# Attention's filler keeps two Strassen products of each of eight gate pairs, and sums of products accumulate in PSUM

## The chip, the cores and the metric

One core of one Trainium2 chip. The metric is the device time of one launch in microseconds (us). The core's engines run side by side, each through its own instruction list in a fixed order, and wait for each other by semaphores: TensorE (PE, with its weight loads shown as PEld), VectorE (DVE), ScalarE (ACT), GpSimd (POOL) and SyncE (SP, which here issues DMAs). Matrix products land in PSUM banks of 128 x 512 fp32 numbers; DVE and ACT read them from there.

## The reference, cut to what matters

```python
def encoder_layer(x, ...):                        # a prompt of 512 tokens, then a sample of 1024
    h = rmsnorm(x, norm_g)
    proj = h @ w_in                               # 1024 -> 4352 + 1024 columns
    qa, ka, va, za, qb, kb, vb, zb, ga, gb = split(proj)
    oa = neighbourhood_attention(qa, ka, va, rpb_a) * silu(za) @ w_o_a   # (after q, k norms)
    ob = window_gqa_attention(qb, kb, vb, t5_table, sink_b) * silu(zb) @ w_o_b
    merged = sigmoid(ga) * oa + sigmoid(gb) * ob  # ga, gb: 1024 columns each
    return x + merged @ w_out
```

Everything is fp32. `z` below stands for za and zb, "gates" for ga and gb, "out" for the product with w_out.

## The kernel before, in words

Everything is kept transposed, with features on the 128 partitions and tokens along the free axis. Two batches follow each other: the prompt (0 to about 395 us) and the sample (from there to the end). The change concerns the sample, which has four stages: attention (about 396 to 785 us), z and the gates (785 to 960), the merge, which multiplies with w_o and the gates (960 to 1083), and out (1083 to the end).

**Precision.** An fp32 operand is split into a rounded part (hi, made by ACT) and a remainder (lo, source minus hi, made by DVE or POOL). `product` (L1276) multiplies a weight block with 512 tokens over k: for each of four k-steps three matmuls of 512 columns, hi x hi (L1284), hi x lo (L1285) and lo x hi (L1286). A product of half of k is thus 12 matmuls into one bank. In the profile `hh`, `hl` are h's parts, `whi`, `wlo` the weights', `fh`, `fl` the filler's weights, and `T` the parts of sums of blocks of h.

**Pairs in Strassen form.** Two blocks of 128 output features by two halves of the tokens by two halves of k make a 2x2 block product. `pair_strassen` (L1320) computes it in seven products (Strassen's scheme in Winograd's form) instead of eight. Products 0 and 1 take plain blocks of weights and of h. Products 2 to 6 need four sums of weights (`S`, 512 columns each, L1161) or the four sums T0 to T3 of h; product 6 takes a sum of weights and plain h. In before each product goes into its own bank; then ACT copies product 0 out (L1354, `U`), and DVE adds (L1161, `U<-U,x` and `C<-U,x`) join the products in SBUF: three partial sums and four results, seven adds in a pair. Results get their sigmoid from ACT (L1387) and are stored in DRAM (`g_d`). In the sample three z pairs, six gate pairs and two out pairs have this form; the rest is plain.

**Sums of h.** T0 to T3 are computed at the start, where the norm is (`norm_pair`), and stored in `t_d`; the dense stage loads them as `U` and splits them into `T` (`stored_sums`, L1237, L1167 and L1172), in the order T1, T2, T0, T3.

**The filler.** Attention leaves gaps on PE while its softmax runs. `fill_gates` fills them with gate products of four of the sixteen gate blocks, two halves of the tokens each: 8 products over the whole k, 24 matmuls each, into one bank `d` that serves the filler alone in this stage. ACT or DVE drains the bank into the one buffer `fc` (L1493), which is stored in `g_d` (L1394). These blocks' pairs are left out of the gates stage; the sigmoid follows when the merge loads them.

**Order.** Nothing is scheduled at run time. A planner (`Flow.run`) takes each operation with a cost, a priority and what it depends on, simulates the engines and writes the operations out in the order of that plan; `f.value` gives a tile from a ring of a stated number of buffers, and a new tile waits until the readers of the one that had the buffer are done. Dense products rotate over eight banks (`ROTA`: two `p`, five `x`, one `d`).

Of the kernel before, what the change touches and what calls it, by code (L numbers as in the profile page):

```python
# [25 lines left out]
FILL_P, FILL_S = 3, 2  # L26
# [14 lines left out]
P = 128  # L41
# [313 lines left out]
def encoder_kernel(  # L355
# [207 lines left out]
    def norm_pair(pool, x_t, rb, hh, hl, t, t_d, prio, load_prio):  # L563
# [572 lines left out]
    def dense_phase(geo, hh, hl, h_ops, o_stores, exps_done, start, opened, tp, up, p0, p1, p2, x_t, y_t, classic, fill, after_gates=None, side=None):  # L1136
# [10 lines left out]
        g_d = dpool.tile([2, 8, P, nt], F32, tag=f"g_d{nt}", name=f"g_d{nt}")  # L1147
        stores = {}
# [36 lines left out]
        def sums(prio, done):  # L1185
# [3 lines left out]
            for k in range(4):  # L1189
# [27 lines left out]
                step(3, lambda v=t[1]: v.t[:, :sn], (1, 0), 0, ALU.subtract, True, t[1])  # L1217
                step(3, lambda v=t[3]: v.t[:, :sn], (1, 0), 1, ALU.subtract, False)
# [57 lines left out]
        def product(ps, ws, movs, prio, first, last, after=(), n=nh):  # L1276

            o = None
            for k, ((hi, lo, c, wops), (mh, ml, mops, mv)) in enumerate(zip(ws, movs)):

                def emit(e, k=k, hi=hi, lo=lo, c=c, mh=mh, ml=ml):
                    out = ps.t[:, :n]
                    cs = slice(c, c + P)
                    pe.matmul(out, hi.t[:, cs], mh(), start=first and k == 0, stop=False)  # L1284
                    pe.matmul(out, hi.t[:, cs], ml(), start=False, stop=False)  # L1285
                    pe.matmul(out, lo.t[:, cs], mh(), start=False, stop=last and k == len(ws) - 1)  # L1286
# [33 lines left out]
        def pair_strassen(srcs, post, prio, mov_h, mov_t, seed=None, last=False):  # L1320
# [19 lines left out]
            def add(out, x, bank, op=ALU.add):  # L1340
                tt(pv(out), pv(x), pv(bank), op, sn, prio, psum=True, new=[out], use=[x, bank])

            def result(m, n, x, bank, op=ALU.add):
                if seed:
                    c = seed(m, n * sn, sn, x, prio)
                    tt(pv(c), pv(c), pv(bank), op, sn, prio, psum=True, use=[c, bank], into=[c])
                else:
                    c = tile_("C", n_c)
                    add(c, x, bank, op)
                post(m, n * sn, sn, c, False, prio)  # L1350

            a = mul(0, mov_h(0, 0))
            f.op(
# [9 lines left out]
            if not last:  # L1363
                result(0, 1, u4, mul(6, mov_h(1, 1)))
                return
# [406 lines left out]
```

## Time and profile before

| | before |
|---|---|
| median of 3 runs (lowest, highest) | 1146.3 us (1145.42, 1147.29) |
| span of the profiled execution | 1144.7 us |
| PE, PEld, DVE, ACT, POOL busy, whole span | 99%, 86%, 75%, 56%, 27% |
| granted clock of TensorE, every slice | 9 or more tenths |
| DMA moved | 159.86 MB, 140 GB/s in the mean |

The profile is of one execution and gives its span from the first to the last instruction; of its own time it shows nothing beyond that span. The span lies 1.6 us under the median of the runs; that much of a launch is outside it. PE's busy time counts from the start of a matmul to its modelled end, so that matmuls overlap and a busy PE isn't yet PE at its peak: what one matmul costs is read from the distance of two starts. "Idle before" and "waited for" are the engine's time with nothing to do, and what ended it.

### The profile page before, as it was taken

To read this page: it belongs to the slowest core of one execution; us is meant where nothing else is said; L and a number is where in the kernel's file an instruction comes from. 1 tells how busy PE (TensorE), PEld (TensorE's weight loads), DVE (VectorE), ACT (ScalarE), POOL (GpSimd) and SP (SyncE) were. 2 spreads that over 40 slices of the span, in tenths; PEclk is the share of its full clock that TensorE was granted. 3 is DMA by queue.
4 is the path that set the end of the run, shared out by engine and by line. 5 is a ranking of instruction groups with operands and counts; after the bars stand their busy time and mean duration, and the time that the engine had idled before them with its cause. 6 is when DMAs were issued, how large, how long until landed. Compare 5 with 4: busy or idle time off the path is not lost.

```text
span 1144.7 us, 18482 instructions
## 1 busy us (share of the span) xinstructions
PE 1133.8 (99%) x6139; PEld 985.8 (86%) x6139; DVE 854.4 (75%) x1975; ACT 644.9 (56%) x1467; POOL 308.3 (27%) x413
## 2 busy tenths in 40 slices
PE   8999999999999999999999999999999999999998
PEld 6999988888888899999999888888888888788887
DVE  5888798497765468887778888865878755497984
ACT  5777987544433346665678988865534434343320
POOL 3653433000010054343333445330222210132110
PEclk9999999999999999999999999999999999999999
DMA  7854543488786422121221213226657335573072
GB/s 253 273 158 141 181 113 102 115 264 266 232 277 199 165 72 67 25 70 32 71 61 50 56 37 93 56 66 214 218 148 211 129 111 159 200 238 121 29 223 90
DMA packets 124705, 159.86 MB, mean 140 GB/s; under 512 B 28297, under 2 KB 66961, under 8 KB 124610
## 3 DMA queue, kind: packets, MB, share of 16 engines
q1 hardware_dynamic: 124610, 158.69, 45.4%
q8 instruction: 48, 0.79, 0.3%
q14 instruction: 47, 0.39, 0.1%
HBM read 121.93 MB, written 41.44 MB: 143 GB/s over the span
## 4 chain that ended last, share of the span: by engine, by line
PE 94%; DVE 2%; DMA 2%; ACT 1%; POOL 1%; issue 0%; SPq 0%; ACTq 0%; POOLq 0%
PE p L761 25%; PE x L1285 9%; PE x L1286 9%; PE x L1284 9%; PE x L1063 5%; PE x L1026 5%; PE x L934 4%; PE p L1284 4%; PE p L1285 4%; PE d L1284 4%; PE p L1286 4%; PE d L1286 4%; PE d L1285 4%; PE x L861 2%; DMA ot<-u_d 1%; DMA w<-in_w_att_dram 1%
## 5 line engine op out<-in xcount | busy, mean ns | idle before, releaser
L761 PE MATMUL p<-whi,hh 128*128 128x384 f32 x384 | 133.4, 348 | 0.0
L761 PE MATMUL p<-wlo,hh 128*128 128x384 f32 x384 | 133.1, 347 | 0.0
L761 PE MATMUL p<-whi,hl 128*128 128x384 f32 x384 | 132.4, 345 | 0.0
L978 ACT ACTIVATE sb<-sb,mx 128x384 f32<-128x384 f32 (+1 forms) x192 | 107.5, 563 | 22.4 <-DVE mx L969 22.2
L1167 ACT ACTIVATE whi<-raw 128x512 fp32r<-128x512 f32 (+1 forms) x140 | 81.1, 590 | 52.6 <-PE x L1285 26.2
L761 PE MATMUL p<-whi,hb 128*128 128x384 f32 x384 | 107.5, 347 | 0.0
L1172 POOL TENSOR_TENSOR wlo<-raw,whi 128x512 fp32r<-128x512 f32 (+1 forms) x29 | 40.9, 1413 | 242.4 <-ACT whi L1167 130.4
L1284 PE MATMUL x<-hh,whi 128*128 128x512 f32 x264 | 102.7, 389 | 0.0
L1285 PE MATMUL x<-hl,whi 128*128 128x512 f32 x264 | 102.7, 389 | 0.0
L1286 PE MATMUL x<-hh,wlo 128*128 128x512 f32 x264 | 102.7, 389 | 0.0
L1037 DVE TENSOR_TENSOR pp<-x,pp 128x512 fp32r<-128x512 f32 (+1 forms) x136 | 82.6, 638 | 18.9 <-ACT pp L1032 17.8
L1172 DVE TENSOR_TENSOR wlo<-raw,whi 128x512 fp32r<-128x512 f32 (+1 forms) x111 | 70.1, 645 | 30.5 <-ACT whi L1167 30.2
L1285 PE MATMUL x<-T,whi 128*128 128x512 f32 x224 | 87.5, 390 | 0.3 <-DVE T L1172 0.2
L1286 PE MATMUL x<-T,wlo 128*128 128x512 f32 x224 | 87.2, 389 | 0.0
L1284 PE MATMUL x<-T,whi 128*128 128x512 f32 x224 | 87.1, 389 | 0.0
L1032 ACT ACTIVATE pp<-x 128x512 fp32r<-128x512 f32 (+1 forms) x136 | 70.9, 560 | 22.8 <-PE x L1026 21.8
L799 POOL TENSOR_TENSOR rs_r<-rs_v,mhalf 128x4 f32<-128x4 f32 (+1 forms) x72 | 81.7, 1134 | 5.7
L1063 PE MATMUL x<-pp,v 128*128 128x256 f32 (+1 forms) x368 | 77.8, 324 | 0.8 <-DVE pp L1037 0.8
L792 POOL TENSOR_SCALAR rs_v<-ss 128x4 f32<-128x4 f32 (+1 forms) x72 | 26.2, 364 | 187.3 <-DVE ss L785 184.6
L761 PEld LDWEIGHTS p<-whi,hl 128*128 128x128 f32 x384 | 73.0, 190 | 1.3 <-issue 1.0
L761 PEld LDWEIGHTS p<-wlo,hh 128*128 128x128 f32 x384 | 73.0, 190 | 1.0 <-issue 0.5
L761 PEld LDWEIGHTS p<-whi,hh 128*128 128x128 f32 x384 | 73.0, 190 | 0.9 <-issue 0.5
(351 smaller groups left out, 2985.5 us busy)
## 6 DMA issues: line engine op xcount, KB each, us to landing
raw<-in_w_g_dram SPq DMA_DIRECT2D x76, 256.0 KB
w<-in_w_att_dram SPq DMA_DIRECT2D x46, 384.0 KB
ot<-o_d SPq DMA_DIRECT2D x36, 256.0 KB
g_d<-C SPq DMA_DIRECT2D x34, 256.0 KB
raw<-in_w_z_dram SPq DMA_DIRECT2D x32, 256.0 KB
raw<-in_w_out_dram SPq DMA_DIRECT2D x32, 256.0 KB
C<-g_d SPq DMA_DIRECT2D x24, 256.0 KB
out_dram<-C SPq DMA_DIRECT2D x23, 256.0 KB
```

The lines of the kernel that those rows point to most:

```text
L761: pe.matmul(ps.t[:, :GW], part[u](k), mv.t[:, c], start=k == 0 and m == 0, stop=k == KC - 1 and m == 2,)
L799: lambda e: nc.gpsimd.tensor_tensor(r.t[:, :nn], rv.t[:, :nn], mhalf[:, :nn], op=ALU.pow),
L978: act.activation(sb.t[:, :width], sb.t[:, :width], AF.Exp, bias=mx.t[:, i : i + 1], scale=-1.0, accum_out=sm.t[:, i : i + 1],)
L1026: pe.transpose(pt.t[:, u * P : (u + 1) * P], sbs[i].t[:, c * P : (c + 1) * P], ident)
L1032: lambda e, pt=pt, pp=pp, nn=nn: act.activation(pp.t[:, 0, :nn], pt.t[:, :nn], AF.Copy),
L1037: lambda e, pt=pt, pp=pp, nn=nn: dve.tensor_tensor(pp.t[:, 1, :nn], pt.t[:, :nn], pp.t[:, 0, :nn].bitcast(F32), op=ALU.subtract),
L1063: pe.matmul(out(), v.t[:, vs], mv(), start=first, stop=last)
L1167: (("act", ACT_(n)),), lambda e: act.activation(hi(), src(), AF.Copy), prio,
L1172: lambda e: engines[e].tensor_tensor(lo(), src(), hi().bitcast(F32), op=ALU.subtract), prio,
L1284: pe.matmul(out, hi.t[:, cs], mh(), start=first and k == 0, stop=False)
L1285: pe.matmul(out, hi.t[:, cs], ml(), start=False, stop=False)
L1286: pe.matmul(out, lo.t[:, cs], mh(), start=False, stop=last and k == len(ws) - 1)
```

## The change

In the sample the filler now serves all eight gate pairs, and gives each of them two products of half of k instead of computing four blocks whole. For a pair it multiplies weight block (0, 0) with h(0, 0), drains the bank into a new DRAM array `p_d`, goes on accumulating block (0, 1) times h(1, 0) into the same bank, and drains that as the finished result (0, 0) into `g_d`. These are products 0 and 1 of the pair. The filler has 8 x 24 matmuls as before. All eight gate pairs are then in Strassen form, with five products in the gates stage and the kept product 0 loaded from `p_d`.

In every Strassen pair of the sample (z and out too) sums of products now accumulate in PSUM. One bank takes products 0, 2, 3 and 5 one after the other; between them a partial sum is read out, by an ACT copy (z, out) or by a DVE add of the kept product (gates), and the next product waits for that read. A second bank takes product 4 and, after it has been read, product 6. T3 changes its sign so that product 5 can be added. In the last pair of all, the two halves of the last product accumulate in the second bank too.

```diff
-FILL_P, FILL_S = 3, 2
+FILL_P, FILL_S = 3, 8
...
-            (3, (1, 1), (1, 0), (1, 0)),
+            (3, (1, 0), (1, 1), (1, 0)),
...
+        p_d = None if short else dpool.tile([2, 4, P, sn], F32, tag="p_d", name="p_d")
...
-        def pair_strassen(srcs, post, prio, mov_h, mov_t, seed=None, last=False):
+        def pair_strassen(srcs, post, prio, mov_h, mov_t, seed=None, last=False, kept=None):
...
-            w = weight_tiles([raw[0, 0], raw[0, 1], s2, s3, s1, raw[1, 1], s4], 6, prio - 0.5)
-            p1, u2, u3, u4 = (tile_("U", 4, sn) for _ in range(4))
+            first = [] if kept else [raw[0, 0], raw[0, 1]]
+            w = weight_tiles([*first, s2, s3, s1, raw[1, 1], s4], 6, prio - 0.5)
+            w = [None] * (7 - len(w)) + w
+            p1, u2, u3 = (tile_("U", 4, sn) for _ in range(3))
...
-            def mul(i, mov):
-                ps = bank(next(tags))
-                h_reads.append(product(ps, w[i], mov, prio, True, True, [opened], sn))
+            def mul(i, mov, ps=None, after=()):
+                fresh = ps is None
+                ps = ps or bank(next(tags))
+                h_reads.append(product(ps, w[i], mov, prio, fresh, True, [opened, *after], sn, again=not fresh))
                 return ps
...
+            def partial(out, ps):
+
+                if kept:
+                    return tt(pv(out), pv(p1), pv(ps), ALU.add, sn, prio, psum=True, new=[out], use=[p1, ps])
+                return f.op(
+                    (("act", ACT_(sn, False)),), lambda e: act.activation(out.t[:, :sn], ps.t[:, :sn], AF.Copy), prio,
+                    new=[out], use=[ps],
+                )
...
-            a = mul(0, mov_h(0, 0))
-            f.op(
-                (("act", ACT_(sn)),), lambda e: act.activation(p1.t, a.t[:, :sn], AF.Copy), prio, new=[p1], use=[a]
-            )
-            result(0, 0, p1, mul(1, mov_h(1, 0)))
-            add(u2, p1, mul(2, mov_t(1)))
-            add(u3, u2, mul(3, mov_t(2)))
-            b = mul(4, mov_t(0))
-            add(u4, u2, b)
-            result(1, 1, u3, b)
-            result(1, 0, u3, mul(5, mov_t(3)), ALU.subtract)
+            if kept:
+                src, after = kept
+                dma(lambda: nc.sync.dma_start(p1.t[:, :sn], src), 512 * sn, prio - 0.5, new=[p1], after=after)
+                x = mul(2, mov_t(1))
+            else:
+                x = mul(0, mov_h(0, 0))
+                o = partial(p1, x)
+                result(0, 0, p1, mul(1, mov_h(1, 0)))
+                x = mul(2, mov_t(1), x, [o])
+            o = partial(u2, x)
+            z = mul(4, mov_t(0))
+            x = mul(3, mov_t(2), x, [o])
+            o = partial(u3, x)
+            read = result(1, 1, u3, z)
+            x = mul(5, mov_t(3), x, [o])
+            if kept:
+                result(1, 0, p1, x)
+            else:
+                post(1, 0, sn, x, True, prio)
             if not last:
-                result(0, 1, u4, mul(6, mov_h(1, 1)))
+                result(0, 1, u2, mul(6, mov_h(1, 1), z, [read]))
                 return
...
-            for br, m in filled:
+            for br, m in filled if short else filled[::2]:
...
-                for n in halves:
-                    ps = bank("d")
-                    o = product(ps, ws[0], mov(0, n), prio, True, False)
-                    h_reads.append(product(ps, ws[1], mov(1, n), prio, False, True, [o]))
...
+                for n in halves if short else (0,):
+                    ps = bank("d")
+                    o = product(ps, ws[0], mov(0, n), prio, True, not short)
+                    if not short:
+                        o = leave(ps, "p", (br, m), p_d[br, m // 2])
+                    h_reads.append(product(ps, ws[1], mov(1, n), prio, False, True, [o], again=not short))
+                    leave(ps, "g", (br, m, n), g_d[br, m, :, half[n]])
```

What moves, at three places of PE's list. Of each product only the first matmul of a run stands here (three matmuls make a k-step, four steps a product); the number at a row's start is left out, and the rows between two that stand here are the rest of the product named by the first.

PE before, in the gates stage, one pair: seven products in seven banks, each of 12 rows. `T_10453` is T1, `T_10525` T2, `T_10586` T0, `T_10648` T3.

```order
L1284 MATMUL x_11331<-T_10453,whi_11146 128x512 [waits DVE_49,Activation_49]
L1284 MATMUL x_11348<-T_10525,whi_11180 128x512 [waits DVE_49,Activation_49]
L1284 MATMUL x_11369<-T_10586,whi_11180 128x512 [waits DVE_49,Activation_49]
L1284 MATMUL x_11391<-T_10648,whi_11215 128x512 [waits DVE_49,Activation_49]
L1284 MATMUL x_11415<-hh_3330,whi_11254 128x512 [waits DVE_49,Activation_49]
```

PE now, in the gates stage, products of two pairs: `d_11225` and `p_11313` are the two banks of one pair, `p_11357` and `x_11439` of the next. `T_10527` is T1, `T_10600` T2, `T_10666` T0, `T_10719` T3.

```order
L1290 MATMUL p_11313<-T_10666,whi_11166 128x512 [waits Activation_49]
L1290 MATMUL d_11225<-T_10600,whi_11150 128x512 [waits DVE_49]
L1290 MATMUL p_11357<-T_10527,whi_11287 128x512 [waits Activation_49]
L1290 MATMUL d_11225<-T_10719,whi_11212 128x512 [waits DVE_49]
L1290 MATMUL p_11313<-hh_3331,whi_11212 128x512 [waits DVE_49]
L1290 MATMUL p_11357<-T_10527,whi_11287 128x512
L1290 MATMUL x_11439<-T_10666,whi_11300 128x512 [waits Activation_49]
L1290 MATMUL p_11357<-T_10600,whi_11287 128x512 [waits DVE_49]
L1290 MATMUL x_11475<-T_10527,whi_11412 128x512 [waits Activation_49]
L1290 MATMUL p_11357<-T_10719,whi_11349 128x512 [waits DVE_49]
```

A pair's products on one bank now wait for DVE's read of it, and other products lie between them: 12 rows of T1 for another pair are cut in two, 6 rows ahead of the pair's product 5 and 6 behind its product 6.

PE before, at the start of z: T1 first, 24 rows of plain products ahead of it, then T2, T0 and T3.

```order
L1284 MATMUL x_10541<-hh_3330,whi_9967 128x512 [waits PE_49]
L1284 MATMUL x_10572<-hh_3330,whi_9967 128x512 [waits PE_49]
L1284 MATMUL x_10611<-T_10453,whi_10044 128x512 [waits PE_49,Activation_49]
L1284 MATMUL d_10634<-T_10525,whi_10417 128x512 [waits Activation_49]
L1284 MATMUL p_10660<-T_10586,whi_10417 128x512 [waits Activation_49]
L1284 MATMUL p_10687<-T_10648,whi_10442 128x512 [waits Activation_49]
```

PE now, at the start of z: T0 (`T_10666`) first, its k-steps mixed with plain products into `d_10677`, then T1 (`T_10527`) and T2 (`T_10600`) on the bank of product 0, `x_10615`.

```order
L1290 MATMUL x_10615<-hh_3331,whi_9925 128x512 [waits PE_49]
L1290 MATMUL x_10646<-hh_3331,whi_9925 128x512 [waits PE_49]
L1290 MATMUL d_10677<-hh_3331,whi_10634 128x512 [waits Activation_49]
L1290 MATMUL x_10694<-T_10666,whi_10493 128x512 [waits PE_49,Activation_49]
L1290 MATMUL x_10694<-T_10666,whi_10493 128x512 [waits Activation_49]
L1290 MATMUL x_10694<-T_10666,whi_10515 128x512 [waits Activation_49]
L1290 MATMUL p_10726<-hh_3331,whi_10634 128x512
L1290 MATMUL x_10615<-T_10527,whi_10026 128x512 [waits Activation_49]
L1290 MATMUL x_10615<-T_10600,whi_10493 128x512 [waits Activation_49]
```

T0 is third in the order of loading. Its use begins 6 rows behind the place where T1's began, instead of 24, and only three rows (`p_10726`) lie between product 2 and product 3 on `x_10615`.

PE before, the end of the program, the last out pair: seven banks, no product follows another on its bank.

```order
L1284 MATMUL x_13376<-T_12811,whi_13230 128x512 [waits DVE_49,Activation_49]
L1284 MATMUL x_13391<-T_12797,whi_13260 128x512 [waits DVE_49,Activation_49]
L1284 MATMUL x_13406<-T_12758,whi_13260 128x512 [waits DVE_49,Activation_49]
L1284 MATMUL d_13423<-T_12828,whi_13292 128x512 [waits DVE_49,Activation_49]
L1284 MATMUL p_13441<-hh_3330,whi_13326 128x256 [waits DVE_49,Activation_49]
L1284 MATMUL p_13456<-hh_3330,whi_13326 128x256 [waits DVE_49]
```

PE now, the end of the program: `p_13333` takes product 2 (T1), 3 (T2) and 5 (T3) of the last pair, `x_13425` product 4 (T0) and the two halves of product 6.

```order
L1290 MATMUL p_13333<-T_12853,whi_13272 128x512 [waits Activation_49]
L1290 MATMUL x_13425<-T_12800,whi_13306 128x512
L1290 MATMUL p_13333<-T_12839,whi_13306 128x512 [waits Activation_49]
L1290 MATMUL p_13333<-T_12870,whi_13342 128x512 [waits Activation_49]
L1290 MATMUL x_13425<-hh_3331,whi_13368 128x256 [waits DVE_49]
L1290 MATMUL x_13425<-hh_3331,whi_13368 128x256
```

Product 5 now follows product 3 on the same bank with nothing between them, and waits for ACT's copy of what product 3 completed.

## Rows read from the trace of the kernel before

**Rows 1.** Chain that ended last, shares of the span by engine.
```profile
PE 94%; DVE 2%; DMA 2%; ACT 1%; POOL 1%; issue 0%; SPq 0%; ACTq 0%; POOLq 0%
```

**Rows 2.** Windows: start:end, length, busy us per engine, clock, DMA share, GB/s.
```profile
396.00:785.00 389.00, 387.40 (x2482) 353.92 (x2481) 309.44 (x877) 273.50 (x696) 151.09 (x221) 1.00 0.23 61
785.00:960.00 175.00, 175.00 (x773) 144.90 (x773) 123.34 (x190) 75.08 (x143) 30.56 (x20) 1.00 0.56 175
...
960.00:1083.00 123.00, 122.66 (x539) 100.72 (x538) 94.71 (x139) 46.71 (x78) 21.29 (x14) 1.00 0.49 159
1083.00:1144.70 61.70, 58.62 (x270) 48.83 (x269) 40.39 (x63) 11.60 (x23) 7.81 (x6) 1.00 0.44 145
```

**Rows 3.** Waits of PE and PEld: us in total, times, longest.
```profile
PE x L1063 <- DVE pp L1037: 0.8, 2, 0.6
PE x L861 <- DVE qk L816: 0.5, 1, 0.5
PE x L1026 <- DVE sb L1010: 0.3, 1, 0.3
...
PEld x L1285 <- DVE T L1172: 1.4, 3, 0.5
```

**Rows 4.** Timeline of PE in the gates stage: start, us.
```profile
816.55 0.39 PE L1284 MATMUL x<-hh,whi 128*128 128x512 f32 x1
...
818.59 0.39 PE L1284 MATMUL x<-hh,whi 128*128 128x512 f32 x1
```

**Rows 5.** Timeline in the merge, around two waits for T's lower part.
```profile
975.01 0.69 DVE L1172 TENSOR_TENSOR T<-ot,T 128x512 fp32r<-128x512 f32 x1 [0.67 <-ACT T L1167]
...
975.15 0.40 PE L1284 MATMUL x<-T,whi 128*128 128x512 f32 x1
...
975.76 0.50 PE L1285 MATMUL x<-T,whi 128*128 128x512 f32 x1 [0.22 <-DVE T L1172]
...
976.10 0.40 PE L1286 MATMUL x<-T,wlo 128*128 128x512 f32 x1
...
979.91 0.40 PE L1286 MATMUL x<-T,wlo 128*128 128x512 f32 x1
...
980.14 0.39 PE L1284 MATMUL d<-T,whi 128*128 128x512 f32 x1
...
980.34 0.69 DVE L1161 TENSOR_TENSOR C<-x,C 128x512 f32<-128x512 f32 x1 [0.83 <-PE x L1286]
```

**Rows 6.** Tile U: count, ns min/median/max, first and last start.
```profile
L1161 DVE TENSOR_TENSOR U<-U,x x21: 674/683/689, 815.4 to 1136.1; 128x512 f32<-128x512 f32 x21
...
L1354 ACT ACTIVATE U<-x x8: 579/599/599, 812.3 to 1125.3; 128x512 f32<-128x512 f32 x8
```

**Rows 7.** Timeline at the start of z: T's parts, first use, product 0's copy.
```profile
805.67 0.39 PE L1284 MATMUL x<-T,whi 128*128 128x512 f32 x1
...
808.36 1.28 ACT L1167 ACTIVATE T<-U 128x512 fp32r<-128x512 f32 x2 [2.62 <-DMA U<-t_d]
...
809.02 1.34 DVE L1172 TENSOR_TENSOR T<-U,T 128x512 fp32r<-128x512 f32 x2 [2.17 <-ACT T L1167]
...
812.34 0.60 ACT L1354 ACTIVATE U<-x 128x512 f32<-128x512 f32 x1
```

**Rows 8.** Window at the start of z, columns as in rows 2.
```profile
785.00:800.00 15.00, 15.00 (x67) 12.39 (x67) 9.60 (x16) 7.76 (x15) 0.00 (x0) 1.00 1.00 336
```

**Rows 9.** Tile S in the gates stage, columns as in rows 6.
```profile
L1172 DVE TENSOR_TENSOR wlo<-S,whi x41: 412/685/1727, 785.8 to 950.6; 128x512 fp32r<-128x512 f32 x24, 128x256 fp32r<-128x256 f32 x17
...
L1161 DVE TENSOR_TENSOR S<-S,raw x7: 693/1666/1669, 800.1 to 932.9; 128x512 f32<-128x512 f32 x7
...
L1161 POOL TENSOR_TENSOR S<-raw x6: 1499/1620/1622, 821.3 to 932.4; 128x512 f32<-128x512 f32 x6
```

**Rows 10.** Tile d in attention: the filler's drains, and who waited for the bank.
```profile
L1493 ACT ACTIVATE fc<-d x4: 598/599/601, 597.0 to 777.5; 128x512 f32<-128x512 f32 x4
L1493 DVE COPY fc<-d x4: 670/692/692, 678.2 to 758.5; 128x512 f32<-128x512 f32 x4
...
DVE fc L1493: 1.7, 3
```

More of the change, by code (lines that the diff above doesn't have):

```diff
@@ L1216, in sums @@
                 step(1, lambda v=t[1]: v.t[:, :sn], (1, 1), 1, ALU.add, False)
-                step(3, lambda v=t[1]: v.t[:, :sn], (1, 0), 0, ALU.subtract, True, t[1])
-                step(3, lambda v=t[3]: v.t[:, :sn], (1, 0), 1, ALU.subtract, False)
+                after = done[k + 4, 0] if done else []
+                tt(
+                    lambda v=t[3]: v.t[:, :sn], h[1, 0, 0], lambda v=t[1]: v.t[:, :sn], ALU.subtract, sn, prio,
+                    new=[t[3]], use=[t[1]], after=after, hold=[hh],
+                )
+                step(3, lambda v=t[3]: v.t[:, :sn], (1, 0), 1, ALU.add, False)
                 for j in (0, 2, 1, 3):
@@ L1274, in weight_tiles, with product @@
             return out
-        def product(ps, ws, movs, prio, first, last, after=(), n=nh):
+        def product(ps, ws, movs, prio, first, last, after=(), n=nh, at=0, again=False):
             o = None
@@ L1281, in emit @@
                 def emit(e, k=k, hi=hi, lo=lo, c=c, mh=mh, ml=ml):
-                    out = ps.t[:, :n]
+                    out = ps.t[:, at : at + n]
                     cs = slice(c, c + P)
-                    pe.matmul(out, hi.t[:, cs], mh(), start=first and k == 0, stop=False)
-                    pe.matmul(out, hi.t[:, cs], ml(), start=False, stop=False)
-                    pe.matmul(out, lo.t[:, cs], mh(), start=False, stop=last and k == len(ws) - 1)
+                    more = {"skip_group_check": True} if again else {}
+                    pe.matmul(out, hi.t[:, cs], mh(), start=first and k == 0, stop=False, **more)
+                    pe.matmul(out, hi.t[:, cs], ml(), start=False, stop=False, **more)
+                    pe.matmul(out, lo.t[:, cs], mh(), start=False, stop=last and k == len(ws) - 1, **more)
                 kw = {"new": [ps]} if first and k == 0 else {"into": [ps]}
@@ L1344, in result @@
+            def result(m, n, x, ps):
                 if seed:
                     c = seed(m, n * sn, sn, x, prio)
-                    tt(pv(c), pv(c), pv(bank), op, sn, prio, psum=True, use=[c, bank], into=[c])
+                    o = tt(pv(c), pv(c), pv(ps), ALU.add, sn, prio, psum=True, use=[c, ps], into=[c])
                 else:
                     c = tile_("C", n_c)
-                    add(c, x, bank, op)
+                    o = tt(pv(c), pv(x), pv(ps), ALU.add, sn, prio, psum=True, new=[c], use=[x, ps])
@@ L1369, in pair_strassen @@
                 s = slice(i * nh // 2, (i + 1) * nh // 2)
-                ps = bank(next(tags))
                 movs = [
@@ L1374, in pair_strassen @@
                 ]
-                product(ps, w[6], movs, prio, True, True, n=nh // 2)
+                o = product(z, w[6], movs, prio, False, True, [read], nh // 2, s.start, True)
                 tt(
-                    lambda s=s: c.t[:, s], lambda s=s: c.t[:, s], lambda ps=ps: ps.t[:, : nh // 2], ALU.add, nh // 2,
-                    prio, psum=True, use=[ps], hold=[c], after=c.writers[:],
+                    lambda s=s: c.t[:, s], lambda s=s: c.t[:, s], lambda s=s: z.t[:, s], ALU.add, nh // 2,
+                    prio, psum=True, hold=[c, z], after=[*c.writers[:], o],
                 )
@@ L1517, in dense_phase @@
             br, m0 = i // 4, 2 * (i % 4)
-            if (br, m0) in filled:
+            if (br, m0) in filled and short:
                 if side:
@@ L1526, in dense_phase @@
             else:
-                pair_strassen(srcs, post, 4 + i, mov_h, mov_t)
+                kept = (p_d[br, m0 // 2], stores["p", br, m0]) if (br, m0) in filled else None
+                pair_strassen(srcs, post, 4 + i, mov_h, mov_t, kept=kept)
             if side:
```

15 lines of the change are left out of this document (8 added, 7 removed).

## The prediction

> **What bounds the kernel now.** I read the chain that ended last first: 94% of the span is PE [rows 1]. No other engine holds more than 2%, so the time is the number of matmuls by their pitch, plus the places where PE stands still. The windows by stage say how large those places are [rows 2]. In z and the gates (785 to 960) PE is busy 175.00 of 175 us; in the merge 122.66 of 123; in attention 387.40 of 389; in the last stage 58.62 of 61.7, most of which is the tail behind the last matmul. DVE is at 80% in attention (309.44 of 389) and 70% in the gates (123.34 of 175). The clock column is 1.00 in every window, the higher of the two levels (2.4 GHz), with PE at work in all of them, so I price no change of the clock. The waits come next [rows 3]: in attention PE waited 1.6 us for DVE in all, in the gates for nothing, and at the start of the merge for DVE's lower parts of T (1.4 us on the weight loads). The time can thus fall only if PE gets fewer columns to stream, and it rises by each new wait that PE runs into.
>
> **What a matmul and a wait cost.** The mean of 389 ns that groups of instructions show overlaps with the next. The pitch is the distance of two starts: 816.55 to 818.59 is 2.04 us for 9 matmuls of 512 columns, 0.2267 us each [rows 4]. A wait is read from the merge [rows 5]. DVE's split ends at 975.01 + 0.69 = 975.70 and the waiting matmul starts at 975.76: 0.06 from DVE's end to PE. The next matmul starts 0.34 later instead of 0.23: each wait costs 0.11 beyond its length. In the other direction the last matmul of a bank starts at 979.91, the next slot is 980.14, and DVE's read of the bank starts at 980.34: 0.20 behind that slot. With 0.68 for DVE's add and 0.60 for ACT's copy [rows 6], the round trip from PE through the bank's reader and back takes 0.20 + 0.68 + 0.06 = 0.94 us with DVE and 0.86 with ACT, if the reader is free at once. Matmuls for other banks must cover it: four (0.91) nearly do for DVE, six (1.36) leave 0.42.
>
> **Matmuls removed.** In before the six gate pairs have 7 products of 12 matmuls, 504 in all. Now eight pairs have 5 products, 480. The filler has 8 times 24 matmuls before and after, and the z and out pairs keep 84 each. So 24 matmuls of 512 columns go, 24 x 0.2267 = 5.44 us, all on the path that sets the end, since PE waits for nothing where they stood.
>
> The Trainium skill would price them lower. "TensorE: Matmul & The Clock Gate", section "Back-to-back issue gap", gives 131 ns for one matmul of 512 columns in a stream of weight loads and matmuls; by that the gain would be 3.1 us and the sum below 2.3 higher. The starts above disagree with the page: nine matmuls in a row never come near its spacing, so it gets no chance of its own.
>
> **DVE, ACT, POOL, SP.** In the gates DVE's adds fall from 6 x 7 = 42 to 8 x 5 = 40 and ACT's 6 copies of product 0 go. In each z pair 7 adds and a copy become 3 adds and 3 copies. The weights of two more pairs need 8 more sums S; the operands to split are 42 before and 40 now. The filler reads 16 weight tiles instead of 8, so 8 more splits, and drains 16 banks instead of 8, at 0.60 us on ACT or 0.69 on DVE [rows 10]. None of these engines is the bound and the sums differ by few instructions, so I count no cost for their load; what they cost as the reader of a bank comes below. DMAs: 8 weight loads for the filler, 8 more for the gates, 8 stores and 8 loads of the kept products, 32 x 256 KB = 8.4 MB. At 336 GB/s, the rate of a full window [rows 8], that is 25 us of the queue, in windows whose share of DMA is 0.23 and 0.56 [rows 2]; hidden by the matmuls there. A kept product is loaded long after its store. SP gets 32 issues more, with nothing urgent behind them except at the start of z.
>
> **Waits added, place by place.** A product that accumulates on a bank now stops PE in order: whatever is queued behind it, products of other pairs that are ready included, stands too.
>
> Gates. The tightest place of each pair is product 5 behind product 3: six matmuls of another pair lie between, 1.36 us against a round trip of 0.94, so 0.42 us are left for DVE to be late, eight times. DVE's list has a split of weights (0.69 [rows 9]) in front of that add, which waits for ACT alone. Product 3 has twelve matmuls ahead of it. The windows show DVE idle 30% of this stage. I take 0.2 us for all eight together; bounds 0 and, with DVE late as in the third rival, 5.4.
>
> Start of z. T0 is used earlier. The first use of T in before starts at 805.67 [rows 7], at the 24th matmul behind the second product; up to it both lists have the same number of rows. T0's third k-step is now 15 rows behind that place, its lower part 16 rows: 805.67 + 16 x 0.2267 = 809.30. DVE finished that lower part at 809.02 + 0.67 = 809.69, after ACT had waited 2.62 us for the DMA [rows 7]. So PE waits 809.75 - 809.30 = 0.45, and 0.11 for the restart: 0.56. Product 2 on the first pair's bank waits for ACT's copy, which ended at 812.34 + 0.60 = 812.94, and its row comes at 813.15 at the earliest: nothing. Product 3 there has three matmuls ahead, 0.68 against 0.86: 0.18 + 0.11 = 0.29. Together 0.85. Below it is 0, if T0's loads come earlier since SP's list differs; above 2.5, if they are 1.65 later: the DMA share is 1.00 there [rows 8].
>
> Last out pair. Product 5 follows product 3 on the same bank with nothing between. PE stands for the whole round trip through ACT: 0.86 + 0.11 = 0.97 us. No work is left to hide it, and it is the surest of the costs. The two half products at the end now wait for DVE's read of the second bank, with twelve matmuls before them: nothing.
>
> Attention. Sixteen drains of the one filler bank instead of eight, and the eight new ones are in the middle of a product pair, where PE must come back. The tightest has 1.20 us of other matmuls (the rows of PE's list by their pitches) against 0.94 with DVE free; but DVE is busy 80% of this stage. In before DVE stood ready at three of its four drains (1.7 us of waiting for the bank in all [rows 10]). I take 0.4 us; bounds -1.5 (the filler is spread over more places and could close the 1.6 us of idle time) and +2 (eight drains, each a quarter of a microsecond late).
>
> The merge starts behind the same 48 matmuls of the last gate products as before, so its 1.4 us of waits stay: 0, bounds -0.7 and +1.5, about half or the whole of them.
>
> **Sum.** -5.44 + 0.2 + 0.85 + 0.97 + 0.4 + 0 = -3.0 us. The profiled execution's span is 1144.7; the new one 1141.7. The runs of before have a median 1.6 above that span, so 1146.3 - 3.0 = 1143.3 us is the forecast, with 1141.8 to 1144.8 as its own range.
>
> **Rivals.** First, the covers hold: T0's loads land in time, DVE is on time, attention loses nothing, and only the last pair pays. -5.44 + 0.97 = -4.5, and as low as -6.0 with attention's idle time closed: 1140.3 to 1141.8. For it: no wait of PE in the gates in before, and DVE's idle 30%. Against it: T0's third step, whose lateness comes from a DMA that is queued behind others.
>
> Second, the gain is eaten: T0's loads 1.65 late (2.5), drains late (2.0), the gates 0.5 and the last pair 0.97 make 6.0 against 5.44: 1146.9, no change. For it: the windows of DMA and of DVE where this happens are the busiest there are. Against it: PE's list has six matmuls or more at all tight places but the three priced above, and DVE was ready for the drains of before.
>
> Third, slower: DVE's add between products 3 and 5 comes late in every gate pair, since an instruction with two SBUF operands in front of it is stretched while POOL works. The tile S shows it: `S<-S,raw` takes 0.693 at the least and 1.666 in the median, 0.97 more; a lower weight part took up to 1.727; POOL's own sums take 1.62 [rows 9]. An add that reads one operand from PSUM is not stretched (0.674 to 0.689 in 21 cases [rows 6]). One stretched instruction in front of each add costs 0.97 - 0.42 + 0.11 = 0.66 a pair, 5.3 in eight: 1148.6. Two cost 1.63 a pair, 13.0 in eight: 1156.3. It decides from a mean lateness of 0.69 us on (3.0 / 8 + 0.42 - 0.11). For it: eight S sums more, some of which may go to POOL, which delays DVE more. Against it: POOL is busy 30.56 of 175 us, so an instruction of DVE meets it one time in six; and the split ahead of the add waits for ACT, not in a crowd.
>
> The Trainium skill has the rule behind this rival: "SBUF — State Buffer", section "Who interferes with whom", says that a VectorE instruction with two SBUF inputs contends with a GpSimd instruction that reads SBUF and the later one blocks wholly, while one with at most one SBUF input doesn't. The rows on tile S and tile U agree with it (1.666 beside 0.683), and it speaks against a change that lets PE wait for DVE in eight more pairs.
>
> **Chances.** Forecast 0.50 (1141.8 to 1144.8); covers hold 0.19; gain eaten 0.19 (1144.8 to 1148.6); slower 0.12. A measurement of this kernel can tell about 0.2% from no change, 2.3 us: faster is below 1144.0, slower above 1148.6. About a fifth of the forecast's own range lies above 1144.0. Faster: 0.19 + 0.8 x 0.50 = 0.59; within 0.2%: 0.10 + 0.19 = 0.29; slower 0.12. The range from 1140.3 to 1148.2 leaves out what attention could give beyond the first rival, the upper edge of the second and the third: under 2 in 10.
>
> **What would show it.** 24 fewer PE instructions of 512 columns and a window of the gates stage some 4 to 5 us shorter; PE waits on an ACT copy `U<-p` once near the end, about 0.7 long, and on T0 near 809 us; no wait on `U<-U,x` in the gates. The third rival would show as waits of PE on L1162 in the gates, each behind a long DVE instruction; the second as waits on `fc` in attention and on T. The forecast is wrong if the gates stage shows DVE as the releaser of PE for over 1 us in all, or if attention's end moves by over 1 us.

## The result: 0.35% slower, and the profile after

The changed kernel takes 1151.65 us (median of 20 runs, 1148.1 to 1155.75) against 1147.05 for the kernel before (20 runs): a ratio of 1.0035, 95% interval 1.0023 to 1.0046 (taken over all runs; the two medians alone would give 1.0040). I had forecast 1143.3, with 1140.3 to 1148.2 as the range: the wrong side, and outside it. A second set of runs gave 1.0021 (1.0011 to 1.0031). The profiled execution has a span of 1146.4 us; its run took 1148.51, the second fastest of the 20, so 2.1 us lie outside the span, not 1.6.

The chain that ended last, of the changed kernel, shares by engine; it answers to [rows 1].

```profile
PE 89%; DMA 4%; DVE 3%; ACT 1%; issue 1%; POOL 1%; SPq 0%; DVEq 0%; POOLq 0%; ACTq 0%
```

PE has lost five points of the chain, and DMA and DVE took three of them. Three points are 34 us and the time grew by less than 5: the chain says on whom PE now hangs at some places, and not what it costs. The windows by stage say where. The columns are those of [rows 2].

```profile
396.00:785.00 389.00, 386.83 (x2476) 352.91 (x2475) 312.90 (x894) 277.69 (x711) 147.90 (x212) 1.00 0.26 70
785.00:960.00 175.00, 172.30 (x756) 141.06 (x754) 114.24 (x176) 75.11 (x144) 38.17 (x33) 1.00 0.63 199
960.00:1083.00 123.00, 121.97 (x531) 99.03 (x530) 92.94 (x133) 46.43 (x78) 26.04 (x18) 1.00 0.49 158
1083.00:1146.40 63.40, 58.40 (x267) 48.05 (x265) 34.02 (x55) 13.34 (x27) 6.58 (x5) 0.99 0.43 141
```

In z and the gates PE was busy 175.00 of 175 us; now it is 172.30. DVE's busy time there fell, from 123.34 to 114.24: it is not more work on DVE that holds PE up. The waits of PE, of the changed kernel (us in total, times, longest), answer to [rows 3]: attention first, then z and the gates, then the rest.

```profile
PE x L861 <- DVE qk L816: 1.6, 3, 1.0
...
PE d L1290 <- ACT fc L1513: 0.2, 1, 0.2
...
PE x L1290 <- DVE U L1162: 2.6, 2, 1.9
...
PE p L1290 <- ACT U L1354: 0.7, 1, 0.7
PE x L1290 <- ACT U L1354: 0.7, 1, 0.7
PE x L1291 <- DVE T L1173: 0.4, 2, 0.2
PE d L1290 <- ACT T L1168: 0.3, 1, 0.3
PE d L1291 <- DVE T L1173: 0.2, 1, 0.2
```

Four of these wait for a reader of a bank that the next product accumulates on: 2.6 us on DVE's adds (`U`, L1162) in the gates, 0.7 twice on ACT's copies (L1354) in the two out pairs. What such a wait hangs on is read from the timeline of the changed kernel in the gates.

```profile
858.27 2.12 POOL L1173 TENSOR_TENSOR wlo<-S,whi 128x256 fp32r<-128x256 f32 x2 [1.86 <-ACT whi L1168]
...
859.36 1.58 DVE L1162 TENSOR_TENSOR ot<-ot 128x512 f32<-128x512 f32 x1 [1.62 <-DMA ot<-o_d]
860.86 0.68 DVE L1173 TENSOR_TENSOR wlo<-S,whi 128x512 fp32r<-128x512 f32 x1
861.47 1.05 DVE L1162 TENSOR_TENSOR C<-C,ot 128x512 f32<-128x512 f32 x1
862.44 0.67 DVE L1162 TENSOR_TENSOR C<-U,x 128x512 f32<-128x512 f32 x1
863.04 0.41 DVE L1173 TENSOR_TENSOR wlo<-S,whi 128x256 fp32r<-128x256 f32 x1
863.38 0.67 DVE L1162 TENSOR_TENSOR U<-U,x 128x512 f32<-128x512 f32 x1
...
865.62 0.69 DVE L1162 TENSOR_TENSOR ot<-ot 128x512 f32<-128x512 f32 x1 [0.97 <-DMA ot<-o_d]
...
867.36 1.24 DVE L1173 TENSOR_TENSOR wlo<-raw,whi 128x512 fp32r<-128x512 f32 x1
...
859.13 0.39 PE L1292 MATMUL x<-T,wlo 128*128 128x512 f32 x1
...
861.85 0.39 PE L1292 MATMUL x<-T,wlo 128*128 128x512 f32 x1
864.10 0.50 PE L1290 MATMUL x<-T,whi 128*128 128x512 f32 x1 [1.86 <-DVE U L1162]
...
869.25 0.50 PE L1290 MATMUL x<-T,whi 128*128 128x512 f32 x1 [0.78 <-DVE U L1162]
```

PE stands at 864.10 for the add `U<-U,x` that starts at 863.38. It is the first such add of the stage: the first gate pair's product 3 waits for the read of what product 2 completed, with the twelve matmuls of product 4 between them. DVE was not idle ahead of it: it works off five instructions one behind the other. But the first, `ot<-ot`, had stood 1.62 us waiting for a DMA of attention's output. It belongs to the posts of the z stage, which run into the gates. It is also stretched, 1.58 instead of 0.69 (the same instruction at 865.62), with POOL at work from 858.27. The second wait, at 869.25, is for product 5 of the same pair and has a like order in front of it: 0.97 us of waiting for the DMA, then a split stretched to 1.24.

How much each part weighs can be worked out for the first wait. Product 2's last matmul starts at 859.13, so the add could have started at 859.36 + 0.20 = 859.56; it came 3.82 later. The twelve matmuls cover 2.72 - 0.94 = 1.78 of that, which leaves 2.04 (2.02 measured). The wait for the DMA is 1.62 of the lateness and the stretch 0.89: without both the add would have come in time, without the DMA's part alone PE would still have stood some 0.4 us, without the stretch alone some 1.2 (estimates from these rows).

In before DVE waited for this DMA too, between 785 and 960, and no matmul waited for DVE.

```profile
DVE ot L1161 <- DMA ot<-o_d: 11.7, 5, 3.9
```

The stretch agrees with what the Trainium skill states on "SBUF — State Buffer", section "Who interferes with whom": an instruction of VectorE with two SBUF inputs contends with one of GpSimd that reads SBUF, and one with at most one SBUF input does not. The adds, which read one operand from PSUM, took no longer with POOL at work (0.68 at 878.20) than without (0.67 at 863.38).

**Where the 3.8 us of the sample come from.** I measure the sample from its first projection matmul to its last matmul, 746.22 us in before (395.13 to 1141.35), 749.49 now (392.97 to 1142.46), and add up by how much the starts of the dense stages' matmuls lie further apart than their pitch: 1.01 us in before, 8.57 now. Then +3.27 = -5.44 for 24 matmuls + 7.56 of standstills + 1.15 that is left for attention. By place: gates 3.38, merge's start 2.89 against 1.01, out pairs 0.92 and 0.95, start of z 0.43. From the last matmul to the end it is 3.94 instead of 3.40 us. Together +3.81. The prompt, whose list on PE is the same, ended 2.16 us earlier in this execution, which makes the span only 1.7 longer.

### The profile page after: what moved, and what is told of

Same layout as the page of the kernel before. It is cut to its first block, busy times and chain, and to the rows that moved or that the text cites. A ratio compares the mean times of both kernels' runs of the same rounds, so it can differ in the third digit from the quotient of the medians.

```text
span 1146.4 us, 18521 instructions
## 1 busy us (share of the span) xinstructions
PE 1130.1 (99%) x6115; PEld 979.4 (85%) x6115; DVE 840.9 (73%) x1966; ACT 651.0 (57%) x1487; POOL 316.2 (28%) x420
## 4 chain that ended last, share of the span: by engine, by line
PE 89%; DMA 4%; DVE 3%; ACT 1%; issue 1%; POOL 1%; SPq 0%; DVEq 0%; POOLq 0%; ACTq 0%
PE p L761 24%; PE x L1290 8%; PE x L1291 8%; PE x L1292 8%; PE x L1063 5%; PE x L934 5%; PE x L1026 5%; PE d L1290 4%; PE p L1290 4%; PE p L1291 4%; PE p L1292 4%; PE d L1292 4%; PE d L1291 4%; PE x L861 2%; DMA ot<-o_d 2%
## 5 line engine op out<-in xcount | busy, mean ns | idle before, releaser
L1168 ACT ACTIVATE whi<-raw 128x512 fp32r<-128x512 f32 (+1 forms) x124 | 73.8, 607 | 75.5 <-DMA raw<-in_w_g_dram 21.9
L1290 PE MATMUL x<-T,whi 128*128 128x512 f32 x240 | 94.3, 393 | 3.5 <-DVE U L1162 2.6
L1291 PE MATMUL x<-T,whi 128*128 128x512 f32 x240 | 94.0, 392 | 0.4 <-DVE T L1173 0.4
L1292 PE MATMUL x<-T,wlo 128*128 128x512 f32 x240 | 93.6, 390 | 0.0
L1292 PE MATMUL x<-hh,wlo 128*128 128x512 f32 (+1 forms) x240 | 92.6, 386 | 0.0
L1291 PE MATMUL x<-hl,whi 128*128 128x512 f32 (+1 forms) x240 | 92.6, 386 | 0.0
L1290 PE MATMUL x<-hh,whi 128*128 128x512 f32 (+1 forms) x240 | 92.6, 386 | 0.0
L1173 POOL TENSOR_TENSOR wlo<-raw,whi 128x512 fp32r<-128x512 f32 (+1 forms) x23 | 30.4, 1329 | 165.9 <-DMA raw<-in_w_g_dram 111.9
```

Of the source, the lines that this page charges most:

```text
L1168: (("act", ACT_(n)),), lambda e: act.activation(hi(), src(), AF.Copy), prio,
L1173: lambda e: engines[e].tensor_tensor(lo(), src(), hi().bitcast(F32), op=ALU.subtract), prio,
L1291: pe.matmul(out, hi.t[:, cs], ml(), start=False, stop=False, **more)
```

## The experiments

Theory A: PE stands at products that wait for the reader of their bank; the 24 matmuls are a real gain that these waits eat. Theory B: the loss is the filler's, with more drains and more DMA in attention. The table holds all runs: the ratio to before, the sample's length as above, and what the starts in its dense stages lie apart beyond the pitch. Ratios are of all runs of a kernel, the other two columns of its one profiled execution.

| kernel | ratio (95%) | sample, us | standstills, us |
|---|---|---|---|
| before | 1 | 746.22 | 1.01 |
| changed | 1.0035 (1.0023, 1.0046) | 749.49 | 8.57 |
| after_again | 1.0021 (1.0011, 1.0031) | 749.43 | 8.75 |
| all_sbuf | 0.9960 (0.9945, 0.9974) | 740.93 | 0.80 |
| psum_only | 1.0087 (1.0070, 1.0104) | 760.20 | 15.07 |
| gates_sbuf | 0.9998 (0.9988, 1.0009) | 744.38 | 3.58 |
| z_out_sbuf | 1.0005 (0.9996, 1.0015) | 747.83 | 6.93 |
| out_sbuf | 1.0028 (1.0018, 1.0038) | 748.87 | 7.81 |
| no_ot_sum | 1.0032 (1.0020, 1.0044) | 750.60 | 9.36 |
| less_pool | 1.0130 (1.0116, 1.0144) | 760.72 | 18.09 |
| no_ot | 0.9995 (0.9985, 1.0006) | 746.24 | 5.54 |
| ot4 | 1.0091 (1.0078, 1.0104) | 756.51 | 15.72 |
| ot3 | 1.0057 (1.0045, 1.0069) | 753.77 | 12.80 |
| best_z0 | 1.0011 (1.0002, 1.0021) | 749.22 | 7.63 |

**The changed kernel once more** (no edit).

> The changed kernel once more. Theory A (PE stands at products that wait for the reader of their bank): waits of PE on U appear again between 850 and 880 us, near 1108 and near 1136, some 4 to 5 us together, and the time is 1.002 to 1.005 of before. Theory B (the loss is the filler's: more drains and more DMA in attention): the stretch from the sample's first projection to the start of z is 3 us or more longer than before's 405 us, and the waits on U change from run to run.

Measured: ratio 1.0021, sample 749.43. The wait at the same place lasts 1.82 us, the one at the last out pair 0.69, the one near 1108 only 0.2; the second wait in the gates is not there. So the waits do change in part, as B said too, but the 3 us that B wanted in attention are missing: with the standstills and the matmuls taken off, 0.9 us are left for it. One thing is new. After the wait the pitch itself changes. Windows of this execution, columns as in [rows 2]: ahead of the wait, the wait, behind it.

```profile
857.00:861.00 4.00, 4.00 (x19) 3.31 (x18) 2.27 (x2) 1.24 (x3) 2.02 (x2) 1.00 0.62 191
861.00:864.00 3.00, 1.18 (x5) 0.67 (x4) 3.00 (x6) 0.63 (x1) 0.00 (x0) 1.00 0.51 118
864.70:868.10 3.40, 3.40 (x9) 2.67 (x8) 2.72 (x3) 0.99 (x3) 1.25 (x1) 0.51 0.36 111
```

The last window holds 9 matmuls where the first profiled execution has 17 in the same stretch: the granted clock was 0.51, about the lower of the two levels (1.2 GHz), and the pitch 0.43 us instead of 0.227. That adds some 1.7 us to a wait of 2 us. In the first execution the same wait was not followed by it.

**Sums in SBUF again, the filler's kept products left in place.** The diff shows what is computed; in the kernel the old form stands ahead of the new lines and returns.

```diff
-            o = partial(u2, x)
-            z = mul(4, mov_t(0))
-            x = mul(3, mov_t(2), x, [o])
-            o = partial(u3, x)
-            read = result(1, 1, u3, z)
-            x = mul(5, mov_t(3), x, [o])
+            add(u2, p1, mul(2, mov_t(1)))
+            add(u3, u2, mul(3, mov_t(2)))
+            b = mul(4, mov_t(0))
+            add(u4, u2, b)
+            result(1, 1, u3, b)
+            result(1, 0, u3, mul(5, mov_t(3)))
...
+            result(0, 1, u4, mul(6, mov_h(1, 1)))
```

> The filler's kept products stay, but the sums of products are formed in SBUF again, each product in a bank of its own (8 x 6 adds in the gates, 24 matmuls fewer than before). A: no wait of PE on U; 5.4 us less than before but for some 0.7 us in attention: ratio 0.995 to 0.998. B: as slow as the changed kernel, ratio 1.002 to 1.005.

Measured: 1141.26 us, ratio 0.9960, faster than both kernels. Its windows for z and the gates, and all its waits of PE from 785 us on:

```profile
785.00:960.00 175.00, 175.00 (x773) 144.93 (x772) 127.54 (x198) 75.42 (x143) 40.89 (x33) 1.00 0.64 203
...
PE p L1291 <- DVE T L1173: 0.2, 1, 0.2
```

DVE has more to do than in the changed kernel (127.54 against 114.24) and the DMA share is 0.64 beside 0.63, yet PE is busy 175.00 of 175. The sample is 5.29 us shorter than before's; 24 matmuls are 5.44. A's price for them stands, B is refuted: of the filler's cost 0.4 us of this sample are left for attention.

**Accumulating in PSUM alone, with the filler of before.**

```diff
-FILL_P, FILL_S = 3, 8
+FILL_P, FILL_S = 3, 2
...
-            for br, m in filled if short else filled[::2]:
+            for br, m in filled:                # and both halves of the tokens, whole k, one drain, as in before
```

> The filler of before (four blocks whole), with sums accumulating in PSUM in the z, gate and out pairs; as many matmuls as before. A: the waits of the changed kernel without its gain: ratio 1.003 to 1.008. B: as before, ratio 0.999 to 1.002.

Measured: 1.0087, above A's upper end. The sample is 13.98 us longer, and the standstills 14.06. With no kept product ACT's copies stand between the products of every pair; the four longest lines of PE's waits from 785 us on:

```profile
PE x L1289 <- ACT U L1353: 2.2, 2, 1.5
PE p L1289 <- ACT U L1353: 2.2, 1, 2.2
PE d L1289 <- ACT U L1353: 2.1, 1, 2.1
PE x L1289 <- ACT T L1167: 1.7, 1, 1.7
```

Behind the one at 887.8 the granted clock was 0.50 again (window 888 to 891), and behind the one at 1119.2 the pitch was 0.43 us too: 1.7 us each, which with the restarts is why 8.6 us of listed waits make 14. This execution was the slowest of its six (1160.4 us, median 1155.09).

**One group of pairs at a time.** Three kernels keep the old form, a bank a product, for the gate pairs, for z and out, or for out alone.

```diff
+            if kept:           # gates_sbuf; "if not kept": z_out_sbuf; "if seed": out_sbuf
...
+                return
```

> The changed kernel with the gate pairs' sums formed in SBUF; z and out accumulate in PSUM. A: the 3.2 us of waits on U in the gates are gone, the 1.9 us of the two out pairs stay: ratio 0.997 to 1.000. B: ratio 1.002 to 1.005.

> The changed kernel with the z and the out pairs' sums in SBUF; the gate pairs alone accumulate in PSUM. Theory A: the waits on U in the gates remain, those at the start of z and near the end go: ratio 0.998 to 1.001, at least 2 us above the kernel with all sums in SBUF. Rival (the waits in the gates come from ACT's copies in the z pairs): no wait in the gates, ratio 0.995 to 0.997.

> The changed kernel with the two out pairs' sums formed in SBUF, each product in a bank of its own. Theory A: no wait of PE on U beyond 1090 us, where it lost 0.9 to 1.9 us and the tail 0.6: 1.5 to 2.5 us less than the changed kernel, ratio 1.000 to 1.002. Rival (these waits only take the place of others near the end): as the changed kernel, 1.002 to 1.004.

Measured: gates_sbuf 0.9998, z_out_sbuf 1.0005, out_sbuf 1.0028. The waits of PE on U, of gates_sbuf from 785 us on, of z_out_sbuf between 785 and 960, and of out_sbuf from 785 on:

```profile
PE p L1290 <- ACT U L1354: 0.7, 1, 0.7
PE x L1290 <- ACT U L1354: 0.6, 1, 0.6
```

```profile
PE p L1290 <- DVE U L1162: 2.9, 2, 1.9
```

```profile
PE x L1290 <- DVE U L1162: 3.0, 2, 2.3
...
PE d L1290 <- DVE U L1162: 0.5, 1, 0.5
```

The waits go where the accumulation goes, so the first two ratios speak for A. Against 0.9960 with all sums in SBUF, accumulating costs 0.45% in the gates and 0.38% in z and out. The rival for z_out_sbuf (ACT's copies in z delay the gates) is out: its waits in the gates are as long. out_sbuf is a miss. Its waits near the end are gone and its last matmul is 0.6 us earlier in the sample, but the gates' waits were 0.9 longer in the profiled run, and in the ratio no gain over the changed kernel can be seen.

**What DVE's adds stand behind.** A1: the addition of two ot blocks, which waits for a DMA. A2: DVE instructions that POOL stretches.

```diff
-            ots = [tile_("ot", n_ot) for _ in range(2 if c >= 4 else 1)]
+            ots = [tile_("ot", n_ot) for _ in range(2 if c >= 4 and short else 1)]     # no_ot_sum
```

```diff
-        any_tt = lambda n: (("dve", DVE_(n)), ("pool", POOL_(n)))
+        any_tt = lambda n: (("dve", DVE_(n)), ("pool", (1 if short else 2.5) * POOL_(n)))    # less_pool
```

> The changed kernel without the second half of branch B's output in the sample's z stage: it isn't loaded and not added, so that y lacks it; 512 x 512 numbers fewer a z block. Theory A1 (the adds that PE waits for in the gates stand on DVE behind an addition of two ot blocks, which waits for the DMA of ot): the two waits of 1.9 and 0.8 us on U between 855 and 880 us go down to under 0.5 together, ratio 0.997 to 1.000. Theory A2 (they stand behind DVE work that POOL stretches): they stay, 2 us or more in all, ratio 1.001 to 1.004.

> The changed kernel with POOL's cost in the planner 2.5 times as high in the sample's dense stages: POOL then has 33 operations on S, T and weight parts instead of 76. A1: the waits on U stay, 2 us or more in the gates. A2: they fall to under 0.5 us, ratio 0.997 to 1.000.

Measured: 1.0032 and 1.0130; the waits stayed in both, 3.1 us and 2.0 us on DVE in the gates. A2 falls as the only cause: with fewer operations on POOL, PE still waited 2.0 us at once (the addition of ot in front took 1.01 there, after 0.59 of waiting for the DMA). less_pool's time has other causes too, since the planner made another program of it (PE also waits for T, for weights and for ACT's copies). A1 falls in the form that I gave it. But the timeline of no_ot_sum, on DVE and PE, shows what stands in its place.

```profile
864.69 1.03 DVE L1162 TENSOR_TENSOR C<-C,ot 128x512 f32<-128x512 f32 x1 [2.76 <-DMA ot<-o_d]
865.63 0.68 DVE L1162 TENSOR_TENSOR U<-U,x 128x512 f32<-128x512 f32 x1
...
866.37 0.50 PE L1290 MATMUL x<-T,whi 128*128 128x512 f32 x1 [2.22 <-DVE U L1162]
```

The addition is gone and the multiplication behind it waits for the same DMA, 2.76 us, directly in front of the add, and nothing there is stretched. So A1': DVE waits for ot at whichever instruction reads it first.

**Without ot, and with more buffers for it.**

```diff
+            if c >= 4 and not short:                              # no_ot
+                store("u", (c, a // nh), u_d[c, :, a : a + n], sg, n, prio)
+                return
```

```diff
-        n_c, n_ot = (4, 2) if short else (5, 2)
+        n_c, n_ot = (4, 2) if short else (4, 4)       # ot4, with U's ring at 3; ot3: (4, 3)
```

> The changed kernel without the product of branch B's gate with its attention output in the sample's z stage: no load of ot and no addition or multiplication with it on DVE there, silu(z) alone is stored, so that y is wrong by it. Theory A1' (DVE waits for the DMA of ot, at whichever instruction reads it first, and the add that PE waits for stands behind): the waits on U between 850 and 880 us fall from 2.7 us to under 0.4; 3 us less than the changed kernel, ratio 0.998 to 1.001. Rival A3 (DVE simply has too much work ahead of the add in this stretch, ot or not): a wait of 1 us or more stays.

> The changed kernel with four buffers for ot instead of two in the sample, four for C instead of five and three for U instead of four, all work kept: the loads of ot can be issued a block earlier. A1': DVE's waits for ot, and with them PE's on U, fall to under 1 us in the gates; ratio 0.999 to 1.002. A3: 2 us or more on U stays.

> The changed kernel with three buffers for ot and four for C in the sample. Each block of branch B needs two of ot, so one load of the next can go ahead, the second not. A1': waits on U in the gates between those of the changed kernel and of the one with four buffers, 0.5 to 2.5 us. A3: 2 us or more.

Measured: no_ot 0.9995. No wait of PE is listed in z and the gates, and PE is busy 174.93 of 175 us (172.30 in the changed kernel):

```profile
785.00:960.00 175.00, 174.93 (x772) 144.34 (x771) 99.53 (x161) 76.91 (x148) 38.03 (x33) 1.00 0.54 177
```

The sample is 3.25 us shorter than the changed kernel's, as long as the two waits and their restarts (2.02 + 0.11 + 0.93 + 0.11 = 3.17). So PE's waits hung on DVE's work with ot. But the edit takes away three things at once: the wait for the DMA, the addition that POOL stretches, and the time of the work itself. A1' is shown as a cause, not as the only one: in no_ot_sum the DMA is enough alone, while in z_out_sbuf the first wait has little of it in front.

```profile
860.39 1.29 POOL L1162 TENSOR_TENSOR S<-raw,S 128x512 f32<-128x512 f32 x1 [0.47 <-POOL wlo L1173]
860.48 1.75 DVE L1162 TENSOR_TENSOR ot<-ot 128x512 f32<-128x512 f32 x1 [0.22 <-DMA ot<-o_d]
...
864.42 0.50 PE L1290 MATMUL p<-T,whi 128*128 128x512 f32 x1 [1.95 <-DVE U L1162]
```

There the stretch (1.75 for 0.69) is larger than the wait for the DMA (0.22), and by the same working as above (product 2's last matmul at 859.37, the add at 863.68) some 0.8 us are left for DVE's plain work ahead of the add, as A3 says. No run takes the three apart.

Both buffer variants are slower, 1.0091 and 1.0057; ot4 misses its ratio. In ot4 PE's waits on DVE's adds in the gates are gone, as A1' says, though DVE still waits 3.3 us for ot (8.7 in the changed kernel); with fewer buffers for U and C, PE waits elsewhere. The waits between 785 and 960 of ot4 and of ot3:

```profile
PE x L1290 <- ACT U L1354: 4.2, 3, 2.9
...
```

```profile
PE x L1290 <- DVE U L1162: 2.9, 1, 2.9
PE x L1290 <- DVE C L1162: 1.6, 1, 1.6
PE x L1290 <- ACT U L1354: 1.1, 1, 1.1
```

ot3 is outside the bounds that A1' gave it (4.5 us on DVE, not 0.5 to 2.5). It has a buffer of C less, too, so neither run tells what more buffers for ot alone would give.

**A version with still fewer matmuls**: all sums in SBUF, and the first z pair in Strassen form too.

```diff
-CLASSIC_S = (1, 0, 2)
+CLASSIC_S = (0, 0, 2)
```

> A version meant to beat both: kept products of the filler, all sums in SBUF, and the first z pair in Strassen form too, which takes 12 more matmuls (2.7 us) away. If the eight plain products at the start of z still cover the loads of T: 2 to 3 us less than the kernel with all sums in SBUF, ratio 0.992 to 0.995. If T comes too late, or the eight banks are all held by products that wait for product 0's copy: waits of PE on T or U at 805 to 820 us, ratio 0.996 to 1.000.

Measured: 1.0011; the second branch of the expectation, and worse than it. PE waits 2.8 us for T at 791 us, much earlier than expected, and the stretch behind runs at the lower clock, with a pitch of 0.43 us. With 36 matmuls fewer than before (8.16 us) and 6.62 more of standstills, some 4.5 us of its sample are not explained; the dense stages show no further gaps, so they lie in attention, where PE is busy 384.79 of 389 us (386.83 in the changed kernel); why is open. Best of all kernels stays the one with all sums in SBUF.

## Why the prediction was wrong

The matmuls removed: right. All sums in SBUF gives 5.29 us for 5.44, and the pitch of 0.2267 holds.

The step that failed is the one on the gates: "I take 0.2 us for all eight together", because "DVE's list has a split of weights (0.69 [rows 9]) in front of that add, which waits for ACT alone." The first pair alone measured 3.17 us, the rest of the stage 0.2. The longer of its two waits (2.02 + 0.11) is where the prediction saw no danger: "Product 3 has twelve matmuls ahead of it." The shorter (0.93 + 0.11) is at product 5, with its six. I had looked at one instruction ahead of the add and at DVE's idle share of 30%. I hadn't asked what DVE's idle time waits for, nor that the last posts of z stand in its list when the first pair comes. The trace of before has it: 11.7 us of DVE's waits between 785 and 960 are for the DMA of ot. An idle share that comes from waiting at the head of an in-order list is no slack for what is behind it. The sign that the prediction named for this came: DVE released PE for 2.6 us in the gates, where over 1 us meant wrong.

The upper bound of 5.4 came from the third rival, the stretching by POOL in all eight pairs. A part of its mechanism is there, 0.89 and 0.56 us in front of the two waits of one pair, beside 1.62 and 0.97 of waiting for the DMA, which no rival had.

The merge: taken as 0, with +1.5 as the bound; the trace shows 1.9 more. T's splits are late there. The waits in the gates are not the cause, since no_ot has none and still stands for 3.1 us between 960 and 1010. With sums in SBUF in the gates it is less (gates_sbuf 1.3, all_sbuf 0.8), but ot3 (1.4) and ot4 (0.5) accumulate there as well. So accumulating in the gates is not enough to bring it, and its cause stays open.

The end: the last out pair measured 0.84 + 0.11 = 0.95 against 0.97 forecast, the timeline of the changed kernel in place of [rows 5]:

```profile
1135.78 0.39 PE L1292 MATMUL p<-T,wlo 128*128 128x512 f32 x1
1136.20 0.60 ACT L1354 ACTIVATE U<-p 128x512 f32<-128x512 f32 x1 [4.84 <-PE p L1292]
...
1136.85 0.50 PE L1290 MATMUL p<-T,whi 128*128 128x512 f32 x1 [0.69 <-ACT U L1354]
1137.19 0.40 PE L1291 MATMUL p<-T,whi 128*128 128x512 f32 x1
...
1142.46 0.28 PE L1292 MATMUL x<-hh,wlo 128*128 128x256 f32 x1
1142.77 0.75 DVE L1162 TENSOR_TENSOR C<-C,x 128x256 f32<-128x256 f32 x2 [2.17 <-PE x L1292]
```

The round trip is as worked out: 0.20 behind the next slot, 0.60 for the copy, 0.05 to PE, 0.11 for the restart. Two things were not priced: the other out pair (0.92 here, 0.33 in the second execution), and the last two rows. The two half results share a bank now, and both adds come behind the last matmul, 0.75 us in place of one of 0.42; that is 0.33 of the 0.54 us by which the end is later. In before the last row was:

```profile
1141.66 0.42 DVE L1161 TENSOR_TENSOR C<-C,p 128x256 f32<-128x256 f32 x1 [0.96 <-PE p L1286]
```

The start of z: 0.85 forecast, 0.43 measured. Product 3 behind the copy cost 0.33 for 0.29, product 2 behind its copy 0.1 for nothing; T0 came in time. Attention: 0.4 forecast, 1.15 left over. The listed waits rose by half a microsecond only (1.1 more on qk, 0.2 on a drain, 0.8 less on pp); the rest is open. The clock: I priced none, since no window of before showed it fall; in the second execution it fell behind the longest wait.

The chances: the measured time lies above 1148.6, the place of the third rival, to which I had given 0.12. The second rival had the gain eaten too, but by other terms: T0's loads were in time for its 2.5, the gates cost 3.4 for its 0.5, and the merge and the other out pair were not in it.

Open is why the first set of runs shows 0.35% and the second 0.21%. The prompt ended 2 us earlier in both traces of the changed kernel than in before's; over the fourteen traces its end lies anywhere from 392.9 to 397.7 us, so that a single span tells little of the change.

## What to carry to other kernels

Before a product is made to wait for a reader of its bank, walk back the reader's own list and ask what each instruction there waits for, DMAs first, above all at the first product of a stage, when the posts of the stage before still stand there; idle time of an in-order engine counts as slack only behind its last wait. A separate bank for each product is what lets such waits pass unseen, and here it was worth more than the adds that accumulating in PSUM saves. Split a change that has two parts: one gave 5.3 us, the other took 9.

## What the runs showed of the hardware

A standstill of PE of about 2 us can be followed by a stretch at the lower clock, 9 matmuls at a granted clock of 0.51 and a pitch of 0.43 us, so that the wait costs nearly twice its length. Of two executions of the same program with the same wait, one showed it and one didn't. Over the profiles of all kernels the clock fell behind waits of 1.8 to 2.9 us in six, and it did not fall behind waits of 1.9 to 2.3 us in four (changed, z_out_sbuf, out_sbuf, no_ot_sum).
